# Mixed groups of 64 and 32 slots, and an earlier list of experts, in a hierarchical mixture of experts

## The chip, the cores and the metric

The kernel runs on one core of a Trainium2 chip. The metric is the device time of one execution in microseconds; lower is better. The profile divides the work of the core among TensorE (PE, with its weight loads PEld), VectorE (DVE), ScalarE (ACT), GpSimd (POOL) and SyncE (SP), whose sequencer issues the transfers this document speaks of.

## The reference

One block of a transformer for 512 tokens of width 1024: attention and a state space branch, an output projection with its residual, and a feed-forward part with 64 experts. The change lies in that last part. Each token picks one of 8 groups and in it 2 of 8 experts, so there are 1024 assignments; an expert is a gated unit of width 512:

```python
g_sel = jnp.argmax(g_logits, axis=-1)
e_sel_logits = jnp.take_along_axis(e_logits, g_sel[:, None, None], axis=1)[:, 0]
top_v, top_i = lax.top_k(e_sel_logits, MOE_TOP_K)          # 2 of 8
weights = g_gate[:, None] * jax.nn.softmax(top_v, axis=-1)
eid = g_sel[:, None] * MOE_EXPERTS_PER_GROUP + top_i
...
def expert_block(args):
    xblk, e = args
    hid = jax.nn.silu(xblk @ w_gate[e]) * (xblk @ w_up[e])
    return hid @ w_down[e]
```

All 64 experts' weights are fp32: gate and up 1024 x 512 each, down 512 x 1024, so 6 MB an expert and 384 MB in all.

## The kernel before

The time up to about 860 us goes to attention, the state space branch, the projections and the routing. Then the experts are worked through in groups. An expert has as many token slots as its place says: places 0 to 11 have 64 (the first four, the static ones, are experts 0 to 3; `NS`), places 12 to 63 have 32. The routing makes a list of the experts in the order of their counts (`perm`), so that the fuller ones come to the wide places; tokens beyond the slots are done by an overflow loop at the end. A group fills 128 columns of TensorE: a **pair** has two experts of 64, a **four** four of 32. The order is two pairs, six fours, four pairs, seven fours.

Per group, in TensorE's order: `gate_up` (8 k steps; in each, for gate and for up, one fp32 matmul of 512 columns for every expert, placed by `tile_position` on the expert's own columns of the array), `combine` of the group before (adds its weighted outputs to the tokens, 16 matmuls), `hidden_t` (4 transposes), `slots` of the next group (4 transposes and 4 small matmuls), and `down` (4 k steps of two halves). Every second group a `gather` of 64 matmuls stands ahead of `down`; it picks the token rows of the next two groups with the one-hot table P that `onehot` makes on VectorE. Group 0 and 1 are gathered together, piece by piece between the k steps of their own `gate_up`. In group 0 TensorE also makes the list (`counts`, at k = 4) and puts the routing weights into its order (`turn`, `put`).

The weights come by SP in loads of 1 MB (two k steps of gate and up, or of down, of one expert): six per expert, in the order of `tiles`, group by group, and inside a group by k step. A load needs a free buffer. `room` counts them; `done` sets the buffers of two k steps free when `gate_up` or `down` has issued these, and `fill` then issues as many loads as there is room for:

```python
def done(k, n=n):
    if k % 2:
        free(n)
        fill()
```

On the chip, a load waits until the matmuls have read its buffer. There are 19 buffers for these loads, and 17 from group 1 on (two become the accumulator). A load of an expert that is not static needs the list: SP reads its entry of `perm` (L1220) and then issues (L1252, or L1250 for a load in two halves).

Of the kernel before, what the change touches and what calls it, by code (L numbers as in the profile page):

```python
# [21 lines left out]
NCH = 4  # L22
# [96 lines left out]
def block_kernel(ctx: ExitStack, tc: tile.TileContext, I, out):  # L119
# [1082 lines left out]
    NS, NW, NF = 4, 12, 6  # L1202
    fours = [list(range(i, i + 4)) for i in range(NW, 64, 4)]
    pairs = [list(range(i, i + 2)) for i in range(0, NW, 2)]
# [19 lines left out]
    homes = []  # L1224
    room = {"ewx": 1, "stg": 0, "big": 0}

    def issue():
        n = nxt["i"]
        nxt["i"] += 1
        kind, e, q = tiles[n]  # L1230
        if n == 0:
            home = "ewx"
        elif n == XS:
            home = "stg"
        else:
            home = next(r for r in ("ewx", "stg", "big") if room[r] > (1 if r == "stg" and n < XS else 0))
        room[home] -= 1
        homes.append(home)
        if home == "stg":
            t = [stage(), stage()]  # L1240
        else:
            b = (mt("ewx", [128, 2048], "ew") if home == "ewx" else big("ew")).rearrange("p (k n) -> p k n", k=2)
            t = [b[:, 0], b[:, 1]]
        wt[kind, e, q] = t
        if n + LASTN >= len(tiles):
            return
        src = source(kind, e, q)
        if home == "stg":
            for i in range(2):
                nc.sync.dma_start(t[i], src[:, i])  # L1250
        else:
            nc.sync.dma_start(b, src)  # L1252
# [145 lines left out]
    def onehot(es, cs=range(NCH)):  # L1398
        n, w = len(es), E if es[0] < NW else E // 2
        if 0 in cs:  # L1400
            R["P", es[0]] = mt("P", [128, NCH, 256], "P")
        P = R["P", es[0]][:, :, :n * w]
        for c in cs:
            if es[0] == 0:
                for e in range(n):
                    V.tensor_scalar(P[:, c, e * w:e * w + w], iota1[:, :w], rk1[:, c, e:e + 1], fst[:, 3, c:c + 1],
                                    op0=OP.is_equal, op1=OP.mult)
            else:
                V.tensor_tensor(P[:, c].rearrange("p (e s) -> p e s", e=n),
                                rk1[:, c, es[0]:es[0] + n].unsqueeze(2).to_broadcast([128, n, w]),  # L1410
                                iota1[:, None, :w].to_broadcast([128, n, w]), op=OP.is_equal)
        if es[0]:
            scaled(P)
        return P
# [14 lines left out]
    def route(cl, prev):  # L1429
# [46 lines left out]
        def rk():  # L1476
            V.scalar_tensor_tensor(rk1[:, cs].rearrange("p c e -> p (c e)"), R["rps"][:, cl[0] * E:cl[-1] * E + E], 1.0,
                                   R["ab"][:, cs].rearrange("p c g e -> p (c g e)"), op0=OP.add, op1=OP.mult)
            R["P0"] = onehot(range(4), cl)

        def gat(k):
            if cl[0] == 0:
                gb[k] = side()
            gather_mm(R["P0"][:, :, :128], gb[k][:, :128], k, cl)
# [42 lines left out]

    def weights1():
        V.tensor_copy(R["cnt"], R["rps"][:, 256:256 + E])
# [19 lines left out]
    j = J("V", 0.8, weights1, [j, kj], prio=5, rel=["s"])  # L1549
# [5 lines left out]
    def free(n=1):  # L1555
        for _ in range(n):
            room[homes.pop(0)] += 1
# [15 lines left out]
    def order_tables():  # L1573


        ox = mt("y", [128, 1024], "ox")
        key, i64, w1, lt_ = (ox[:, i * E:i * E + E] for i in range(4))
        bd = ox[:, 512:640]
        kc, pc, cc_ = (ox[:, i:i + 1] for i in (640, 641, 642))
        tT = mt("y", [128, 4, 128], "tT")  # L1580
        V.tensor_scalar(key, R["cnt"], 64.0, None, op0=OP.mult)
        V.tensor_tensor(key, key, iota1, op=OP.subtract)
        V.tensor_scalar(key[:, :NS], iota1[:, :NS], -1.0, 1.0e6, op0=OP.mult, op1=OP.add)
        V.tensor_tensor(i64, ident[:, :E], ident[:, E:], op=OP.add)
        V.tensor_tensor(w1, key, i64, op=OP.mult)
        V.tensor_reduce(kc, w1, axis=AX.X, op=OP.add)
        V.tensor_scalar(lt_, key, kc, None, op0=OP.is_gt)
        V.tensor_reduce(pc, lt_, axis=AX.X, op=OP.add)
        V.tensor_scalar(pc, pc, 1.0, None, op0=OP.add)
        V.memset(bd, 0.0)  # L1590
        for i in range(2):
            r = slice(64 * i, 64 * i + 64)
            V.tensor_scalar(bd[r, 64 * i:64 * i + 64], iota1[r], pc[r], None, op0=OP.is_equal)
# [3 lines left out]
        def counts():  # L1597
            ps = side()
            T.matmul(ps[:1, :E], lhsT=pidx[:E], rhs=bd[:E, :E], start=True, stop=True)
            T.matmul(ps[:, E:2 * E], lhsT=cc_[:E].to_broadcast([E, 128]), rhs=bd[:E, :E], start=True, stop=True)  # L1600
            V.tensor_copy(R["perm"], ps[:1, :E])
            V.tensor_copy(R["cnt"], ps[:, E:2 * E])
# [13 lines left out]
        return {4: counts, 5: turn, 7: put}  # L1616
# [48 lines left out]
    def slots(P, n, w, wcols):  # L1665
        W = n * w
# [6 lines left out]
        for c in range(NCH):  # L1673
            T.matmul(ws[:W, :n], lhsT=P[:, c], rhs=wcols(c), start=(c == 0), stop=(c == 3))
        sl = pools["mp"].tile([128, 1], F32, name="sl", bufs=2)[:W]
        for e in range(n):
            V.tensor_scalar(sl[w * e:w * e + w], ws[w * e:w * e + w, e:e + 1], 0.5, None, op0=OP.mult)
        return pt, sl

    def gate_up(xt, n, w, gu, done=lambda k: None, pre=lambda k: None):  # L1680
        W = n * w
        pg, pu = gps.tile([128, 512], F32, name="g"), gps.tile([128, 512], F32, name="g")
        for k in range(8):
            pre(k)
            for i, o in enumerate((pg, pu)):
                for e in range(n):
# [18 lines left out]
    def down(ht, n, w, dn, done=lambda k: None):  # L1705
        ps = [side(), side()]
        for k in range(4):
            for i in range(2):
                for e in range(n):
                    es_ = slice(w * e, w * e + w)  # L1710
                    T.matmul(ps[i][es_], lhsT=ht[:, k, es_], rhs=dn(e, k)[:, i * 512:i * 512 + 512],  # L1711
                             start=(k == 0), stop=(k == 3), tile_position=(0, w * e))
            done(k)
        return ps
# [26 lines left out]

    def group_slots(P, gi):
        g_ = groups[gi]
        n, o = len(g_), 128 * (gi % 2)
        return slots(P[:, :, o:o + 128], n, 128 // n, lambda c: wtab[:, c, g_[0]:g_[0] + n])
# [4 lines left out]
    nP = [P]  # L1750
    for gi, g_ in enumerate(groups):
        n = len(g_)
        w = 128 // n
        last = gi == NG - 1

        def done(k, n=n):
            if k % 2:
                free(n)
                fill()

        def pre(k):
            if gi < 2 and 1 <= k < 7:
                half = slice(128 * gi, 128 * gi + 128)
                gather(P[:, :, half], xt[:, :, half], [k + 1])
            if gi == 0 and k in ordering:
                ordering[k]()
            if gi == 1 and k == 7:
                nP[0] = onehot(sum(groups[2:4], []))
# [3 lines left out]
        def wk(kind):  # L1772
            return lambda e, k: wt[kind, g_[e], k // 2][k % 2]
# [6 lines left out]
        o = 128 * (gi % 2)  # L1780
        hh = gate_up(xt[:, :, o:o + 128], n, w, wk("gu"), done, pre)
        if gi == 0:
            ps_ = group_slots(P, 0)
        elif not last:
# [7 lines left out]
        if gi % 2 == 0:  # L1792
            if not last:
                ps_ = group_slots(P, gi + 1)
            if gi == 0:
                gather(P[:, :, 128:], xt[:, :, 128:], [0, 1])
            elif gi + 2 < NG:
                nP[0] = onehot(sum(groups[gi + 2:gi + 4], []))
        elif not last:
            P = nP[0]  # L1800
            xt = rows(P.shape[2])
            gather(P, xt)
            ps_ = group_slots(P, gi + 1)
        yps = down(ht, n, w, wk("dn"), done)
# [7 lines left out]
    with tc.For_i(0, nov, 1) as m:  # L1812
# [23 lines left out]
        pt1, sl1 = slots(P1, 1, E, lambda c: cw1[:, c:c + 1])  # L1836
        hh = gate_up(xo, 1, E, lambda e, k: ow["gu", k])
# [3 lines left out]
        combine(pt1, *weighted(down(ht, 1, E, lambda e, k: ow["dn", k]), E, sl1, yo))  # L1841
# [123 lines left out]
```

## Time and profile before

| | |
|---|---|
| time, median of 3 runs | 1846.72 us (1846.01 to 1850.67) |
| the profiled execution | 1846.09 us, span in the trace 1844.3 us, mean granted TensorE clock 0.955 |
| TensorE busy | 1655.2 us (90%) |
| DMA | 474.68 MB, mean 257 GB/s over the span |
| expert loads, issue to landing | 18.3 us (gate/up), 18.6 us (down) |

The busy share is a mean over stages of different kinds. The page's line of GB/s, in 40 slices, shows where the stream of weights runs at its full rate and where it does not; a timeline of SP shows when loads are issued, and one of TensorE what it does between the reads that set buffers free.

### The profile page before, as it was taken

The page shows a single profiled execution, that of the slowest core. Times are in us where ns is not written, and L with a number is a line of the kernel's source. Part 1 is how long each engine was busy: PE and PEld are TensorE (multiplying, and loading weights), DVE is VectorE, ACT ScalarE, POOL GpSimd, SP SyncE. Part 2 cuts the span into 40 slices and gives each one's busy share as a digit, 9 for nine tenths or more (in the row PEclk, how much of TensorE's full clock was granted, in tenths as well). Part 3 has the DMA queues.
Part 4 walks back from the last instruction along what each step waited for, and adds up shares of the span by engine and source line. Part 5 has one row for each costly group of instructions (what it writes and reads, how often), then busy time and mean ns, then how long its engine had stood idle before and what let it go on. Part 6 is the DMA issues. An engine that isn't in the chain of part 4 may idle for free. (4 is left out here: it accounts for less than half of the span.)

```text
span 1844.3 us, 23121 instructions
## 1 busy us (share of the span) xinstructions
PE 1655.2 (90%) x8831; PEld 1033.7 (56%) x8831; DVE 788.4 (43%) x1499; ACT 424.8 (23%) x877; POOL 316.9 (17%) x329
## 2 busy tenths in 40 slices
PE   7999999999999999999996977769999787697775
PEld 6877788878787777887551423224455242142322
DVE  7698832587878865335230521021322212012113
ACT  5355530344444432121110100001111010010002
POOL 5244421253635352110000000000000000000001
PEclk9999999999999999999998998889999999898887
DMA  5321122212122122369869999999999999999994
GB/s 163 98 66 49 47 92 92 76 62 85 58 87 64 63 80 92 103 227 370 319 250 421 420 421 420 420 420 420 420 420 420 420 420 420 421 420 421 419 420 187
DMA packets 81329, 474.68 MB, mean 257 GB/s; under 512 B 10176, under 2 KB 10560, under 8 KB 35392
## 3 DMA queue, kind: packets, MB, share of 16 engines
q1 hardware_dynamic: 81216, 473.17, 64.9%
q8 instruction: 71, 1.16, 0.3%
q14 instruction: 42, 0.34, 0.1%
HBM read 471.04 MB, written 2.10 MB: 257 GB/s over the span
## 5 line engine op out<-in xcount | busy, mean ns | idle before, releaser
L1688 PE MATMUL g<-ew,xt 128*32 128x512 f32 (+1 forms) x1920 | 401.1, 691 | 131.8 <-DMA ew<-in_gu_dram 131.8
L243 PE MATMUL g<-hH,w 128*128 128x512 f32 x1024 | 345.7, 401 | 0.0
L1688 PEld LDWEIGHTS g<-ew,xt 128*32 128x32 f32 (+1 forms) x1920 | 96.0, 128 | 418.1 <-DMA ew<-in_gu_dram 237.6
L243 PEld LDWEIGHTS g<-hH,w 128*128 128x128 f32 x1024 | 192.4, 188 | 43.7 <-issue 5.9
L1693 DVE SCALAR_TENSOR_TENSOR hh<-hh,g 128x512 f32<-128x512 f32 x19 | 13.1, 688 | 457.4 <-ACT hh L1692 457.4
L243 PE MATMUL g<-hL,w 128*128 128x512 f32 x512 | 199.9, 390 | 0.0
L1711 PE MATMUL s<-ew,hT 128*32 128x512 f32 (+1 forms) x960 | 166.7, 640 | 20.2 <-DMA ew<-in_dn_dram 19.5
L1867 POOL TENSOR_TENSOR fst<-fst 128x1 f32<-128x1 f32 x4 | 1.2, 302 | 977.7 <-ACT fo L1860 977.7
L203 DVE TENSOR_TENSOR w<-stg,w 128x1024 fp32r<-128x1024 f32 x108 | 141.9, 1322 | 55.9 <-ACT w L200 33.2
L1422 PE MATMUL s<-P,x 128*128 128x256 f32 (+1 forms) x704 | 138.8, 355 | 0.0
L1422 PEld LDWEIGHTS s<-P,x 128*128 128x128 f32 x704 | 120.0, 192 | 24.2 <-issue 9.7
L1692 ACT ACTIVATE hh<-g 128x512 f32<-128x512 f32 x19 | 11.3, 597 | 476.2 <-PE g L1688 476.2
L198 POOL TENSOR_SCALAR w<-stg 128x1024 fp32r<-128x1024 f32 x60 | 70.5, 1175 | 255.0 <-DMA stg<-in_wu_dram 159.6
L1711 PEld LDWEIGHTS s<-ew,hT 128*32 128x32 f32 (+1 forms) x960 | 44.3, 121 | 125.0 <-issue 80.5
L243 PEld LDWEIGHTS g<-hL,w 128*128 128x128 f32 x512 | 96.4, 188 | 16.9
L1733 DVE TENSOR_TENSOR acc<-acc,s 128x512 f32<-128x512 f32 x144 | 88.0, 679 | 26.6 <-PE s L1728 26.6
L1721 DVE SCALAR_TENSOR_TENSOR yl<-s,sl,yh 128x512 fp32r<-128x512 f32 x38 | 28.5, 751 | 152.5 <-ACT yh L1720 151.1
L848 DVE SCALAR_TENSOR_TENSOR xb<-u,cw,xb 128x511 f32<-128x511 f32 (+2 forms) x96 | 81.7, 861 | 23.4 <-ACT xb L844 21.7
L243 PE MATMUL g<-w,hH 128*128 128x512 f32 x256 | 84.5, 411 | 0.0
L200 ACT ACTIVATE w<-stg 128x1024 fp32r<-128x1024 f32 x60 | 63.2, 1053 | 76.4 <-DMA stg<-in_wu_dram 53.8
L243 PE MATMUL g<-sH,w 128*128 128x512 f32 x256 | 80.0, 393 | 0.0
L1720 ACT ACTIVATE yh<-s,sl 128x512 fp32r<-128x512 f32 x38 | 26.1, 687 | 188.6 <-PE s L1711 187.5
(333 smaller groups left out, 2383.3 us busy)
## 6 DMA issues: line engine op xcount, KB each, us to landing
ew<-in_gu_dram SPq DMA_DIRECT2D x240, 1024.0 KB, 18.3
ew<-in_dn_dram SPq DMA_DIRECT2D x116, 1024.0 KB, 18.6
stg<-in_wu_dram SPq DMA_DIRECT2D x120, 512.0 KB, 3.6
stg<-in_gu_dram SPq DMA_DIRECT2D x32, 512.0 KB, 17.6
stg<-in_dn_dram SPq DMA_DIRECT2D x16, 512.0 KB, 17.4
xT<-in_xT_dram SPq DMA_DIRECT2D x4, 512.0 KB, 5.8
x<-in_xn_dram SPq DMA_DIRECT2D x2, 1024.0 KB, 10.9
ew<-in_dn_dram SPq DMA_DIRECT2D x4, 512.0 KB, 13.0
```

What stands on the lines that cost most here:

```text
L198: G.tensor_scalar(c["h"], c["st"], 1.0, 0.0, op0=OP.mult, op1=OP.add)
L200: A.activation(c["h"], c["st"], AF.Copy)
L203: (G if i % 10 == 9 else V).tensor_tensor(c["lo"], c["st"], c["h"].bitcast(F32), op=OP.subtract)
L243: T.matmul(cell[b], lhsT=x, rhs=y, start=first and i == 0, stop=last and i == 2)
L848: V.scalar_tensor_tensor(x()[:, 3 - k:], t["u"][:, :n], w[:, k:k + 1], x()[:, 3 - k:], op0=OP.mult, op1=OP.add)
L1422: T.matmul(o, lhsT=x1(c)[:, d], rhs=P[:, c], start=(c == 0), stop=(c == NCH - 1))
L1688: T.matmul(o[es_], lhsT=xt[:, k, es_], rhs=gu(e, k)[:, i * 512:i * 512 + 512], start=(k == 0), stop=(k == 7), tile_position=(0, w * e))
L1693: V.scalar_tensor_tensor(hh, hh, 1.0, pg[:W], op0=OP.add, op1=OP.mult)
L1711: T.matmul(ps[i][es_], lhsT=ht[:, k, es_], rhs=dn(e, k)[:, i * 512:i * 512 + 512], start=(k == 0), stop=(k == 3), tile_position=(0, w * e))
L1720: A.activation(yh[:, i], ps[i][:W], AF.Copy, scale=sl[:, :1])
L1721: V.scalar_tensor_tensor(yl[:, i], ps[i][:W], sl[:, :1], yh[:, i].bitcast(F32), op0=OP.mult, op1=OP.subtract)
L1733: V.tensor_tensor(res(c)[:, h], src(c)[:, h], ps, op=OP.add)
```

## The change

Every group but the first and the fours is now one expert of 64 slots and two of 32 (T below); the order is one pair, then T and F (a four) as the string says. Three experts are static. The list of experts is made by jobs of the routing (`order0` to `order2`) that TensorE and VectorE take before group 0. Buffers are set free by tile. Group 0 is gathered alone; the rows of groups 1 and 2 are gathered together between group 0's `down` and group 1's `gate_up`, and later gathers stand ahead of `down` in even groups.

```diff
-    NS, NW, NF = 4, 12, 6
-    groups = pairs[:NS // 2] + fours[:NF] + pairs[NS // 2:] + fours[NF:]
+    NS, NW = 3, 12
+    groups = [[0, 1]]
+    wide = list(range(2, NW))
+    for kind in "TFTFTTFTFTFTTFTFTF":
+        groups.append([wide.pop(0)] + some(2) if kind == "T" else some(4))
...
-        tiles += [("gu", e, q) for q in range(4) for e in g_] + [("dn", e, q) for q in range(2) for e in g_]
+        first = [e for e in g_ if e < NS]
+        for es in (first, g_[len(first):]):
+            tiles += [("gu", e, q) for q in range(4) for e in es] + [("dn", e, q) for q in range(2) for e in es]
...
+    def onehot(gs):
+        P = mt("P", [128, NCH, 256], "P")[:, :, :128 * len(gs)]
+        for i, g_ in enumerate(gs):
+            for w in (64, 32):
+                es = [e for e in g_ if width(e) == w]
+                if es:
+                    o = 128 * i + (128 - 32 * len(es) if w == 32 else 0)
+                    for c in range(NCH):
+                        V.tensor_tensor(P[:, c, o:o + w * len(es)].rearrange("p (e s) -> p e s", s=w),
...
+        scaled(P)
...
         def rk():
-            R["P0"] = onehot(range(4), cl)
+            for c in cl:
+                for e in range(2):
+                    V.tensor_scalar(R["P0"][:, c, 64 * e:64 * e + 64], iota1, rk1[:, c, e:e + 1], fst[:, 3, c:c + 1],
...
+    def order1():
+        V.tensor_copy(R["cnt"], R["rps"][:, 256:256 + E])
+        V.scalar_tensor_tensor(key, R["cnt"], 64.0, io, op0=OP.mult, op1=OP.subtract)
+        V.tensor_scalar(key[:, :NS], io[:, :NS], -1.0, 1.0e6, op0=OP.mult, op1=OP.add)
+        V.tensor_tensor(w1, key, i64, op=OP.mult)
+        V.tensor_reduce(kc, w1, axis=AX.X, op=OP.add)
+        V.tensor_scalar(lt_, key, kc, None, op0=OP.is_gt)
+        V.tensor_reduce(pc, lt_, axis=AX.X, op=OP.add)
+        for i in range(2):
+            r = slice(64 * i, 64 * i + 64)
+            V.tensor_scalar(ox[r, 512 + 64 * i:576 + 64 * i], io[r], pc[r], None, op0=OP.is_equal)
+
+    def order2():
+        R["ops"] = side()
+        T.matmul(R["ops"][:1, :E], lhsT=pidx[:E], rhs=R["ox"][:E, 512:576], start=True, stop=True)
...
+    oj = J("V", 1.8, order1, [kj, oj], prio=0.5, rel=["s"])
+    oj = J("P", 0.3, order2, [oj], prio=12, acq=["s"], lag=0.2)
+    J("V", 0.2, lambda: V.tensor_copy(R["perm"], R["ops"][:1, :E]), [oj], prio=0, rel=["s"], lag=0.2)
...
-    def free(n=1):
-        for _ in range(n):
-            room[homes.pop(0)] += 1
+    def free(tl_):
+        room[homes[tl_]] += 1
...
-        return {4: counts, 5: turn, 7: put}
+        return {3: turn, 5: put, 6: counts}
...
             for i, o in enumerate((pg, pu)):
-                for e in range(n):
-                    es_ = slice(w * e, w * e + w)
-                    T.matmul(o[es_], lhsT=xt[:, k, es_], rhs=gu(e, k)[:, i * 512:i * 512 + 512],
-                             start=(k == 0), stop=(k == 7), tile_position=(0, w * e))
+                for e, r in es:
+                    T.matmul(o[r], lhsT=xt[:, k, r], rhs=gu(e, k)[:, i * 512:i * 512 + 512],
+                             start=(k == 0), stop=(k == 7), tile_position=(0, r.start))
...
-            if gi < 2 and 1 <= k < 7:
-                half = slice(128 * gi, 128 * gi + 128)
-                gather(P[:, :, half], xt[:, :, half], [k + 1])
+            if gi == 0:
+                if 1 <= k < 7:
+                    gather(P, xt[:, :, :128], [k + 1])
...
         if gi == 0:
             ps_ = group_slots(P, 0)
+            P = onehot(groups[1:3])
...
+        if gi == 0:
+            xt = rows(256)
+            gather(P, xt)
+            ps_ = group_slots(P, 1)
```

`down` has the same edit as `gate_up`; `slots` now multiplies by 64 columns of the weight table where it took 2 or 4.

On TensorE, the end of the routing and the first k steps of group 0 before (L1422 are gathers, L1688 gate/up, L1599 makes the list):

```order
L303 MATMUL s<-ident 128x128 x4
L1422 MATMUL s<-P,x_7000 128x128 x4
L1688 MATMUL g<-ew,xt 64x512 x4
L1422 MATMUL s<-P,x_6945 128x128 x2
L1422 MATMUL s<-P,x_7000 128x128 x2
L1688 MATMUL g<-ew,xt 64x512 x4
...
L1599 MATMUL s<-ox,pidx 1x64
L1600 MATMUL s<-ox 128x64
L1688 MATMUL g<-ew,xt 64x512 x4
```

and of the change (L1436 gathers, L1715 gate/up, L1570 makes the list):

```order
L303 MATMUL s<-ident 128x128 x4
L1436 MATMUL s<-P,x_7000 128x128 x4
L1570 MATMUL s<-ox,pidx 1x64
L1715 MATMUL g<-ew,xt 64x512 x4
L1436 MATMUL s<-P,x_6945 128x128 x2
L1436 MATMUL s<-P,x_7000 128x128 x2
L1715 MATMUL g<-ew,xt 64x512 x4
```

The matmul that makes the list has moved from between the fourth and fifth k step of group 0 to ahead of the first.

On TensorE again, from group 0's down to group 1's gate/up, before (L1711 down, L1688 gate/up with gathers between its steps):

```order
L1711 MATMUL s<-ew,hT 64x512 x16
L1688 MATMUL g<-ew,xt 64x512 x4
L1422 MATMUL s<-P,x_6945 128x128 x2
L1422 MATMUL s<-P,x_7000 128x128 x2
L1688 MATMUL g<-ew,xt 64x512 x4
```

and of the change (L1737 down, L1436 gather, of which 16 such rows of 2 stand here, L1697 and L1702 the slots of group 1, L1715 gate/up):

```order
L1737 MATMUL s<-ew,hT 64x512 x16
L1436 MATMUL s<-P,x_6945 128x256 x2
L1436 MATMUL s<-P,x_7000 128x256 x2
...
L1697 MATMUL s<-ident,P 128x128 x4
L1702 MATMUL s<-ptab,P 128x64 x4
L1715 MATMUL g<-ew,xt 64x512
L1715 MATMUL g<-ew,xt 32x512 x2
L1715 MATMUL g<-ew,xt 64x512
L1715 MATMUL g<-ew,xt 32x512 x2
```

A whole gather for two groups has come between, and the matmuls of a k step change width twice per half.

On SP, the loads around the first read of the list, before:

```order
L1252 DMA ew<-in_gu_dram 128x2048 x8
L1252 DMA ew<-in_dn_dram 128x2048 x4
L1220 TENSOR_LOAD perm
L1252 ISA
L1252 DMA ew<-in_gu_dram 128x2048
L1220 TENSOR_LOAD perm
```

and of the change:

```order
L1270 DMA ew<-in_gu_dram 128x2048 x4
L1270 DMA ew<-in_dn_dram 128x2048 x2
L1238 TENSOR_LOAD perm
L1270 ISA
L1270 DMA ew<-in_gu_dram 128x2048
L1238 TENSOR_LOAD perm
```

Six loads of the fourth static expert are gone from ahead of the first read, which now follows 18 loads instead of 24.

## Rows read from the trace of the kernel before

**Rows 1.** The page: span, and GB/s in 40 equal slices of it.

```profile
span 1844.3 us, 23121 instructions
...
GB/s 163 98 66 49 47 92 92 76 62 85 58 87 64 63 80 92 103 227 370 319 250 421 420 421 420 420 420 420 420 420 420 420 420 420 421 420 421 419 420 187
```

**Rows 2.** Windows: length, busy us PE, PEld, DVE, ACT, POOL, clock, DMA share, GB/s.

```profile
864.00:963.00 99.00, 98.96 (x580) 53.23 (x577) 22.48 (x54) 15.87 (x33) 0.00 (x0) 1.00 0.69 270
948.00:1800.00 852.00, 701.74 (x3834) 292.85 (x3830) 180.33 (x351) 70.60 (x128) 0.00 (x0) 0.92 1.01 420
```

**Rows 3.** Waits of SP's queue, 862 to 948: total us, times, longest.

```profile
SPq L1252 <- PE g L1688: 46.6, 6, 17.6
SPq L1252 <- PE s L1711: 33.6, 4, 22.2
```

**Rows 4.** Timeline of SP, 785 to 950: start, us, issues of loads merged (xN).

```profile
817.08 2.49 SPq L1252 DMA_DIRECT2D ew<-in_gu_dram  x5
...
835.13 32.84 SPq L1252 DMA_DIRECT2D ew<-in_gu_dram  x8
868.06 12.73 SPq L1252 DMA_DIRECT2D ew<-in_dn_dram  x4
881.71 0.35 SPq L1252 DMA_DIRECT2D ew<-in_gu_dram  x1
...
909.16 37.64 SPq L1252 DMA_DIRECT2D ew<-in_gu_dram  x7
```

**Rows 5.** Timeline of TensorE, group 0: two k steps of gate/up.

```profile
862.72 1.94 PE L1688 MATMUL g<-ew,xt 128*64 128x512 f32 x8
...
865.68 1.94 PE L1688 MATMUL g<-ew,xt 128*64 128x512 f32 x8
```

**Rows 6.** Timeline of TensorE, groups 1 and 2: gather, down, gate/up of a four.

```profile
924.12 14.08 PE L1422 MATMUL s<-P,x 128*128 128x256 f32 x64
...
939.36 7.09 PE L1711 MATMUL s<-ew,hT 128*64 128x512 f32 x32
...
949.42 10.90 PE L1688 MATMUL g<-ew,xt 128*32 128x512 f32 x98
```

**Rows 7.** Timeline of VectorE: P and list of group 0, later P.

```profile
859.76 1.87 DVE L1406 TENSOR_SCALAR P<-iota,ptab,fst 128x64 f32<-128x64 f32 x8
...
866.46 0.53 DVE L1593 TENSOR_SCALAR ox<-iota,ox 64x64 f32<-64x64 f32 x2
...
916.17 1.43 DVE L1409 TENSOR_TENSOR P<-ptab,iota 128x256 f32<-128x256 f32 x4 [16.07 <-PE s L1422]
```

**Rows 8.** Transfers issued from 867 to 868: KB, us to landing.

```profile
ew<-in_gu_dram SPq DMA_DIRECT2D x1, 1024.0 KB, 4.7
```

**Rows 9.** Timeline of TensorE, 987 to 994.9, a four's k step that waits for loads.

```profile
989.72 1.04 PE L1688 MATMUL g<-ew,xt 128*32 128x512 f32 x2 [1.45 <-DMA ew<-in_gu_dram]
992.09 1.86 PE L1688 MATMUL g<-ew,xt 128*32 128x512 f32 x2 [1.32 <-DMA ew<-in_gu_dram]
994.58 1.08 PE L1688 MATMUL g<-ew,xt 128*32 128x512 f32 x4 [0.63 <-DMA ew<-in_gu_dram]
```

**Rows 10.** Timelines of TensorE and its weight loads, from pair to four.

```profile
944.56 1.89 PE L1711 MATMUL s<-ew,hT 128*64 128x512 f32 x8
946.38 0.62 PE L1688 MATMUL g<-ew,xt 128*32 128x512 f32 x1
...
945.42 0.14 PEld L1711 LDWEIGHTS s<-ew,hT 128*64 128x64 f32 x2 [0.28 <-issue]
946.37 0.11 PEld L1688 LDWEIGHTS g<-ew,xt 128*32 128x32 f32 x1 [0.81 <-issue]
```

**Rows 11.** Timeline of weight loads, the two other changes of width.

```profile
1286.90 0.13 PEld L1688 LDWEIGHTS g<-ew,xt 128*64 128x64 f32 x1 [0.84 <-issue]
...
1422.64 0.11 PEld L1688 LDWEIGHTS g<-ew,xt 128*32 128x32 f32 x1 [0.81 <-issue]
```

**Rows 12.** Weight loads at the change from group 0's down to group 1.

```profile
897.96 0.14 PEld L1688 LDWEIGHTS g<-ew,xt 128*64 128x64 f32 x2 [0.29 <-issue]
```

More of the change, by code (lines that the diff above doesn't have):

```diff
@@ L1197, in block_kernel, with some, width, spans @@
     give("big", 8, [wsl])
-    NS, NW, NF = 4, 12, 6
-    fours = [list(range(i, i + 4)) for i in range(NW, 64, 4)]
-    pairs = [list(range(i, i + 2)) for i in range(0, NW, 2)]
-    groups = pairs[:NS // 2] + fours[:NF] + pairs[NS // 2:] + fours[NF:]
-    NG = len(groups)
+    NS, NW = 3, 12
+    narrow = iter(range(NW, 64))
+    def some(n):
+        return [next(narrow) for _ in range(n)]
+    groups = [[0, 1]]
+    wide = list(range(2, NW))
+    for kind in "TFTFTTFTFTFTTFTFTF":
+        groups.append([wide.pop(0)] + some(2) if kind == "T" else some(4))
+    NG = len(groups)
+    def width(e):
+        return 64 if e < NW else 32
+    def spans(g_):
+        o = 0
+        for e in g_:
+            yield e, slice(o, o + width(e))
+            o += width(e)
     tiles = []
     for g_ in groups:
-        tiles += [("gu", e, q) for q in range(4) for e in g_] + [("dn", e, q) for q in range(2) for e in g_]
+        first = [e for e in g_ if e < NS]
+        for es in (first, g_[len(first):]):
+            tiles += [("gu", e, q) for q in range(4) for e in es] + [("dn", e, q) for q in range(2) for e in es]
     wt = {}
@@ L1237, in issue @@
         room[home] -= 1
-        homes.append(home)
+        homes[kind, e, q] = home
         if home == "stg":
@@ L1598, in counts @@
             ps = side()
[L1599 to L1602, printed above, removed]
+            T.matmul(ps[:, :E], lhsT=cc_[:E].to_broadcast([E, 128]), rhs=bd[:E, :E], start=True, stop=True)
+            V.tensor_copy(R["cnt"], ps[:, :E])
         def turn():
@@ L1663, in rows, with slots @@
         return mt("xt", [128, 8, 256], "xt")[:, :, :w]
-    def slots(P, n, w, wcols):
-        W = n * w
+    def slots(P, es, wcols):
+        W = es[-1][1].stop
         ps = side()
@@ L1673, in slots, with gate_up @@
         for c in range(NCH):
[L1674 removed]
+            T.matmul(ws[:W, :E], lhsT=P[:, c], rhs=wcols(c), start=(c == 0), stop=(c == 3))
         sl = pools["mp"].tile([128, 1], F32, name="sl", bufs=2)[:W]
[L1676 to L1677 removed]
+        for e, r in es:
+            V.tensor_scalar(sl[r], ws[r, e:e + 1], 0.5, None, op0=OP.mult)
         return pt, sl
[L1680 to L1681 removed]
+    def gate_up(xt, es, gu, done=lambda k: None, pre=lambda k: None):
+        W = es[-1][1].stop
         pg, pu = gps.tile([128, 512], F32, name="g"), gps.tile([128, 512], F32, name="g")
@@ L1703, in hidden_t, with down @@
         return ht
-    def down(ht, n, w, dn, done=lambda k: None):
+    def down(ht, es, dn, done=lambda k: None):
         ps = [side(), side()]
@@ L1708, in down @@
             for i in range(2):
[L1709 to L1712, printed above, removed]
+                for e, r in es:
+                    T.matmul(ps[i][r], lhsT=ht[:, k, r], rhs=dn(e, k)[:, i * 512:i * 512 + 512],
+                             start=(k == 0), stop=(k == 3), tile_position=(0, r.start))
             done(k)
@@ L1740, in combine, with cols @@
                 combine_add(combine_mm(pt, yh, yl, c, i), c, i, src)
+    def cols(gi):
+        o = 128 * ((gi + 1) % 2) if gi else 0
+        return slice(o, o + 128)
     def group_slots(P, gi):
-        g_ = groups[gi]
-        n, o = len(g_), 128 * (gi % 2)
-        return slots(P[:, :, o:o + 128], n, 128 // n, lambda c: wtab[:, c, g_[0]:g_[0] + n])
+        return slots(P[:, :, cols(gi)], list(spans(groups[gi])), lambda c: wtab[:, c])
     xt, P = xt[0], R["P0"]
@@ L1749, in block_kernel @@
     ordering = order_tables()
-    nP = [P]
     for gi, g_ in enumerate(groups):
-        n = len(g_)
-        w = 128 // n
         last = gi == NG - 1
[L1756 to L1759, printed above, removed]
+        es = list(spans(g_))
         def pre(k):
-            if gi < 2 and 1 <= k < 7:
-                half = slice(128 * gi, 128 * gi + 128)
-                gather(P[:, :, half], xt[:, :, half], [k + 1])
[L1765 to L1768, printed above, removed]
+            if gi == 0:
+                if 1 <= k < 7:
+                    gather(P, xt[:, :, :128], [k + 1])
+                if k in ordering:
+                    ordering[k]()
             elif last and k == 4:
@@ L1772, in wk, with done, f @@
         def wk(kind):
-            return lambda e, k: wt[kind, g_[e], k // 2][k % 2]
+            return lambda e, k: wt[kind, e, k // 2][k % 2]
+        def done(kind):
+            def f(k):
+                if k % 2:
+                    for e in g_:
+                        free((kind, e, k // 2))
+                    fill()
+            return f
         if last:
@@ L1791, in block_kernel @@
         pt, sl = ps_
[L1792 to L1801, printed above, removed]
+        if gi % 2:
+            ps_ = group_slots(P, gi + 1)
+            if not last and gi + 2 < NG:
+                P = onehot(groups[gi + 2:gi + 4])
+        elif gi and not last:
+            xt = rows(256)
             gather(P, xt)
             ps_ = group_slots(P, gi + 1)
-        yps = down(ht, n, w, wk("dn"), done)
+        yps = down(ht, es, wk("dn"), done("dn"))
+        if gi == 0:
+            xt = rows(256)
+            gather(P, xt)
+            ps_ = group_slots(P, 1)
         pend = (pt, *weighted(yps, 128, sl))
```

66 lines of the change are left out of this document (24 added, 42 removed).

## The prediction

> **What bounds the kernel now.** I read the page first, for where the span goes. In its GB/s line (40 slices of 46.1 us) slices 22 to 39 stand at 419 to 421, and the three before them at 370, 319 and 250 [rows 1]. So the second half of the span is the stream of expert weights, and TensorE, busy as it looks, waits for it. The windows say how tight that is: from 948 to 1800 the stream moves 420 GB/s, but between 864 and 963 only 270, while TensorE is busy without a gap at a granted clock of 1.00 [rows 2]. One load of 1 MB (1.0486 million bytes) at 420 GB/s takes 2.50 us. The lull is worth 99 x (1 - 270/420) = 35.4 us of stream, and as all 384 MB must pass, this idle time is what the end waits for; the rest of the stage can't be shortened by TensorE.
>
> Next, who holds the loads back in the lull: between 862 and 948 SP waits 46.6 us for TensorE's gate/up matmuls and 33.6 for its down matmuls, that is, for a buffer to be read out, and not for the list of experts [rows 3]. One load goes out early and eighteen from 817.1 on without a pause; the last of the eight issues from 835.1 to 868.0 is the twentieth, which waits until 867.6, and the run of seven that starts at 909.2 holds the longest pause [rows 4]. TensorE is slow there because it does other work between reads: in group 0 the gathers stand between the k steps (a step is 2.96 us, of it 1.9 gate/up) [rows 5]; after group 1 come combine, a 14.1 us gather for two groups, and only then the down matmuls that free buffers [rows 6].
>
> **The change, part by part.** *Loads.* Bytes, count and size stay: 384 loads. So only idle stream time counts, and the sum is: the profiled execution's 1846.1 us (1.8 outside its span of 1844.3, 0.6 under the median of 1846.7), less 35.4, plus the new idle time.
>
> *List of experts.* Load 19 now needs the list. VectorE makes four compares for P instead of eight from 859.76 on (half of 1.87 us) and then nine short operations; their like took 0.26 us each, so I count 2.2 us [rows 7]: list ready 862.9, TensorE's one matmul, which now stands ahead of group 0, at about 863.1, group 0 at 863.4 instead of 862.7, the copy at 864.0, SP's read and issue 0.9 to 1.3 us on (880.8 to 881.7 is the like case [rows 4]): issued 865.3. A load into an idle queue lands 4.7 us after its issue [rows 8]: 870.0, where 866.8 would be its turn (817.1 + 4.7 + 18 x 2.50). Below, this costs nothing (if it arrives in time); above, 16 us more, if it went out no sooner than the first such load of before (881.7 [rows 4]). I take 3.2, since nothing else stands on that path.
>
> *Group 0* reads two experts as before. Half of its gather is gone from behind its gate/up, but a gather of 14.1 us and the slots (1.4) for groups 1 and 2 now stand between its down and group 1. Steps at 2.96, with the moved table work: gate/up ends 886.9, down 889.9 to 896.8 (7 us as before), gather to 910.9, group 1 at 912.2. VectorE's one-hot tables for that gather are twelve compares and a product; four compares took 1.43 us [rows 7], so I count 5; they lie beside the down matmuls, and each microsecond beyond 896.8 would be a microsecond of delay.
>
> *Groups of 64 + 32 + 32 (call them T).* This decides. Widths that are alike run beside each other: a pair of 64, or four of 32, takes 0.43 us per pass (98 matmuls of a four in 10.9 us [rows 6]). An expert's two passes follow each other: at 989.7 both ran before the next expert's weights landed at 992.1 [rows 9]. No row shows 64 and 32 on different columns at once. The ends: side by side, a half step (512 columns, two passes) is 0.86 us, as for pairs; one after the other, it is the wide expert's two passes, then the narrow two's. The nearest rows are the three places where the width changes between groups. At 946.38 the first 32-wide matmul starts 0.53 us after the last pass of the 64-wide (rounds at 944.56, 944.99, 945.42, 945.85), not 0.43; and its weights are loaded at 946.37, right ahead of it, where the 64-wide ones had theirs one whole pass earlier (945.42 for 945.85) [rows 10]. The same stands at 1422.64 and 1286.90, where the weight loads had been idle for 0.81 and 0.84 us [rows 11], against 0.28 between rounds, while from 64 to 64 the weights at 897.96 were early [rows 12]. In these places the columns overlap, which a T group's don't; but the early loading ends too, so I take it that TensorE finishes one width before it takes up the other. Then a half step is 0.52 + 0.43 + 0.52 + 0.43 = 1.90 us, a T's gate/up (16) 30.5, its down (8) 15.2, in all 25.1 more than side by side.
>
> The Trainium skill's "TensorEngine Tiling (Array Packing)", section Key Properties, says that changing the tiling mode, not just the tile, drains the TensorE. By that rule the sum stays as it is here, since 128x64 and 128x32 are listed as modes of their own; the rows at the three changes agree with it, with 0.10 us (0.53 less 0.43) at 946.38, but only for overlapping columns.
>
> *What a group costs TensorE besides.* Four pair groups took 1286.90 to 1422.64 = 135.7 us with two gathers [rows 11]: (135.7 - 28.2)/4 = 26.9, of it 20.6 matmuls; 6.4 are combine, transposes and slots. So T is 52 us, and its three experts need 18 x 2.50 = 45 us of stream; F is 27, or 41 with a gather, against 60.
>
> *New idle time, followed through the order of the loads.* (1) Load 18 lands at 864.3. Load 33 is the first that group 1's gate/up frees, at its second k step: 912.2 + 4 x 1.90 = 919.8, landed 924.5. Fourteen loads (35 us) lie in these 60.2: 25.2 idle. (2) Group 1's gate/up frees twelve buffers, two of which become the accumulator; its last is read at 942.7, and the first down buffers come after 6.4 + 7.6 us, at 956.7, landed 961.4. Ten loads from 924.5 are done by 947.0; 961.4 - 2.5 - 947.0 = 11.9 idle. (3) Two T's follow each other twice (groups 5 and 6, 12 and 13). From the end of group 4 to the first down buffer of group 6: 52 + 30.5 + 20.4 (combine and gather) + 7.6 = 110.5 us. In this the stream can place 17 buffers plus the 30 that are read, less 4 already landed (12 loads fit into the F's last 31 us, 8 of them its own): 43 loads, 107.5 us. With the 2.2 us of latency: 5 idle. Bounds 0 and 29 (118 of TensorE less 90 of stream for 36 loads). I take 6, and 4 for the second time. (4) Issue gaps of the old lull, some 2. Sum 25.2 + 11.9 + 10 + 2 = 49.1, that is 13.7 more than 35.4: **1846.1 + 13.7 = 1859.8, forecast 1860 us**, slower by 0.7%. Its own range is 1850 (both doubles free, list in time) to 1875 (doubles at half their bound).
>
> **Rivals.** *Side by side (faster).* If disjoint columns of different width run together, group 1 frees load 33 at 912.2 + 4 x 0.86 = 915.6, landed 920.3: 56.0 - 35 = 21.0 idle. Its down buffers come at 912.2 + 13.7 + 6.4 + 3.4 = 935.7, ahead of the stream (945.3), so no idle there, and a T (27, with a gather 41) is under its 45. With 2 of gaps: 23, so 1846.1 - 12.4 = 1834. For it: column groups ran independently at 994.58, where four started together though one of them was the rest of an older round [rows 9]. Against it: the early weights that stop at each change of width. It decides at a half step of about 1.7 us; below this the gain remains. The Trainium skill's "TensorE: Matmul & The Clock Gate", Part 3, The mechanism, has the tile's place in a mask per instruction and lets tiles that don't conflict overlap; read so, it speaks for this rival and would make 1834; rows 9 agree for equal widths and no row shows unequal ones.
>
> *TensorE bounds the whole stage (much slower).* If buffers take up less of the double T's than I count, up to 29 us each come back as idle: 1846.1 + (25.2 + 11.9 + 58 + 2 - 35.4) = 1908. Against it: 17 buffers are 42 us deep, and in the pair stage a group took TensorE 33.9 us (135.7/4 [rows 11]) for 30 us of stream, and the mean over 948 to 1800 is still 420 GB/s [rows 2].
>
> *Nothing measurable.* One width still ends before the other but the next width's weights load early, or the list costs and the smaller lull gains cancel: within 5.5 us of 1846.
>
> **How the numbers follow.** One width after the other as summed 0.52; side by side 0.36; TensorE-bound beyond 1876 0.07; no change 0.05. What this kernel's measurement can tell from no change is about 0.3% (5.5 us). The range reaches from side by side with the list in time (1830) to the doubles at half their bound (1876): it leaves out the TensorE-bound case and some of the edges. Faster: 0.36 and a little of the forecast's and the null's low side, 0.38; same 0.06; slower 0.56.
>
> **What would show it.** In a T group, the 32-wide matmuls start about 0.95 us after the 64-wide one (0.43 + 0.52) and 0.01 us after it if the rival holds; gate/up of group 1 lasts 30 us or 14. The stream's lull ends near 962 with a second dip inside group 1, or near 920. In groups 5 to 6 TensorE is without gaps and SP waits for it. Group 0 starts within 1 us of 862.7 and load 19 is issued near 865. The prediction is wrong if T's half step is not near 1.9 us, or if the gather ahead of group 1 waits for VectorE's tables.

## The result, and the profile after

The change took 1859.42 us (median, 1855.86 to 1861.72) against 1847.57 us for the kernel before on the same chip: a ratio of 1.006, 95% interval 1.0038 to 1.0082, so it is slower by about 12 us. The profiled execution is the fastest of the four, 1855.86 us with a span of 1854.1.

The page of the changed kernel: the span, TensorE's share, and GB/s in 40 slices of 46.4 us.

```profile
span 1854.1 us, 23043 instructions
...
PE 1792.5 (97%) x8767; PEld 1034.0 (56%) x8767; DVE 794.3 (43%) x1566; ACT 422.2 (23%) x869; POOL 317.6 (17%) x329
...
GB/s 158 101 63 52 47 91 91 80 58 91 61 77 74 64 71 100 103 248 367 245 313 421 420 420 420 420 339 421 420 420 420 420 421 415 374 420 420 421 420 255
```

Beside [rows 1], the old lull (367, 245, 313) is there still, and two slices later in the stream have fallen to 339 and 374, which stood at 420. TensorE has gone to 97% busy, though it has 8767 matmul passes where the kernel before has 8831. Windows over these places (us, busy PE, PEld, DVE, ACT, POOL, clock, DMA share, GB/s), of the changed kernel:

```profile
864.00:970.00 106.00, 105.31 (x484) 43.24 (x484) 21.91 (x64) 12.12 (x24) 0.00 (x0) 1.00 0.72 277
970.00:1780.00 810.00, 788.99 (x3576) 289.13 (x3564) 176.84 (x395) 70.07 (x126) 0.00 (x0) 0.99 1.00 413
1140.00:1240.00 100.00, 99.75 (x436) 35.32 (x438) 19.13 (x44) 8.33 (x15) 0.00 (x0) 1.00 0.93 382
1530.00:1620.00 90.00, 89.75 (x393) 29.03 (x392) 19.71 (x42) 7.04 (x12) 0.00 (x0) 1.00 0.97 394
```

and of the kernel before, the same two long stretches:

```profile
864.00:970.00 106.00, 105.87 (x634) 56.87 (x632) 29.39 (x69) 16.46 (x34) 0.00 (x0) 1.00 0.71 280
970.00:1780.00 810.00, 663.19 (x3578) 277.86 (x3576) 165.87 (x324) 69.41 (x126) 0.00 (x0) 0.92 1.01 420
```

Idle stream, at 420 GB/s: in the lull 106 x (1 - 277/420) = 36.1 us against 35.3, and behind it 810 x (1 - 413/420) = 13.5 us against none. So the lull was not shortened and two new dips came. Why, TensorE's timeline of a k step in group 1 shows (start, us, merged matmuls):

```profile
936.97 1.62 PE L1715 MATMUL g<-ew,xt 128*64 128x512 f32 x3
937.98 0.62 PE L1715 MATMUL g<-stg,xt 128*32 128x512 f32 x1
938.42 0.59 PE L1715 MATMUL g<-ew,xt 128*32 128x512 f32 x1
938.43 0.59 PE L1715 MATMUL g<-stg,xt 128*32 128x512 f32 x1
938.95 1.07 PE L1715 MATMUL g<-ew,xt 128*64 128x512 f32 x2
```

and the timeline of its weight loads in the same stretch:

```profile
936.97 0.19 PEld L1715 LDWEIGHTS g<-ew,xt 128*64 128x64 f32 x2 [0.84 <-issue]
937.97 0.11 PEld L1715 LDWEIGHTS g<-ew,xt 128*32 128x32 f32 x1 [0.81 <-issue]
...
938.95 0.19 PEld L1715 LDWEIGHTS g<-ew,xt 128*64 128x64 f32 x2 [0.84 <-issue]
```

The 64-wide pass starts at 936.97, the 32-wide ones of the other columns 1.01 us later, the next 64-wide at 938.95: a half step takes 1.98 us, and no pass of one width runs beside one of the other. The weights of each width are loaded only when the other has ended, after the 0.81 and 0.84 us of idle time that [rows 10, 11] show at the old changes of width.

The lull itself is read from these points of the changed kernel. On TensorE they are the start of group 0, the start of group 1's gate/up, and the first matmul behind it:

```profile
862.99 1.98 PE L1715 MATMUL g<-ew,xt 128*64 128x512 f32 x8
...
911.16 25.44 PE L1715 MATMUL g<-ew,xt 128*64 128x512 f32 x75
...
942.92 0.50 PE L1753 MATMUL s<-yh,pt 128*128 128x512 f32 x1
```

On SP they are the issue of load 19, the first that needs the list, and of the first load whose buffer group 1 frees:

```profile
864.43 0.36 SPq L1270 DMA_DIRECT2D ew<-in_gu_dram  x1
...
919.21 2.01 SPq L1270 DMA_DIRECT2D ew<-in_gu_dram  x3
```

Counted from the first load, the one issued at 919.21 is the 32nd, since the 19 buffers and the twelve that group 0 frees hold 31. The prediction and an expectation below call it load 33. The fourteen loads that the prediction counts behind load 18 end at load 32, so its sum is not changed by this.

### The profile page after: what moved, and what is told of

Same layout as the page of the kernel before. It is cut to its first block, busy times and chain, and to the rows that moved or that the text cites. A ratio compares the mean times of both kernels' runs of the same rounds, so it can differ in the third digit from the quotient of the medians.

```text
span 1854.1 us, 23043 instructions
## 1 busy us (share of the span) xinstructions
PE 1792.5 (97%) x8767; PEld 1034.0 (56%) x8767; DVE 794.3 (43%) x1566; ACT 422.2 (23%) x869; POOL 317.6 (17%) x329
## 5 line engine op out<-in xcount | busy, mean ns | idle before, releaser
L1715 PE MATMUL g<-ew,xt 128*32 128x512 f32 (+1 forms) x1904 | 460.3, 603 | 13.4 <-DMA ew<-in_gu_dram 13.3
L1715 PEld LDWEIGHTS g<-ew,xt 128*32 128x32 f32 (+1 forms) x1904 | 91.9, 114 | 348.5 <-issue 319.0
L1737 PE MATMUL s<-ew,hT 128*32 128x512 f32 (+1 forms) x968 | 245.2, 634 | 13.4 <-DMA ew<-in_dn_dram 12.0
L1737 PEld LDWEIGHTS s<-ew,hT 128*32 128x32 f32 (+1 forms) x968 | 49.2, 119 | 193.7 <-issue 150.9
L1436 PE MATMUL s<-P,x 128*128 128x256 f32 (+1 forms) x640 | 136.3, 372 | 0.0
L1436 PEld LDWEIGHTS s<-P,x 128*128 128x128 f32 x640 | 117.3, 192 | 20.8 <-issue 5.7
L1719 ACT ACTIVATE hh<-g 128x512 f32<-128x512 f32 x19 | 11.3, 597 | 425.1 <-PE g L1715 425.1
## 6 DMA issues: line engine op xcount, KB each, us to landing
ew<-in_dn_dram SPq DMA_DIRECT2D x4, 512.0 KB, 13.7
```

The lines of the kernel that those rows point to most:

```text
L1436: T.matmul(o, lhsT=x1(c)[:, d], rhs=P[:, c], start=(c == 0), stop=(c == NCH - 1))
L1715: T.matmul(o[r], lhsT=xt[:, k, r], rhs=gu(e, k)[:, i * 512:i * 512 + 512], start=(k == 0), stop=(k == 7), tile_position=(0, r.start))
L1737: T.matmul(ps[i][r], lhsT=ht[:, k, r], rhs=dn(e, k)[:, i * 512:i * 512 + 512], start=(k == 0), stop=(k == 3), tile_position=(0, r.start))
```

## The experiments

Two columns below come from the landing times of all expert loads in each profile: how much longer the time from the second landing to the last is than 2.49 us for each 1 MB between them (the stream's idle time, the lull in it), and the time from the last landing to the end of the span (the tail). The difference of two rows says more than a row by itself, which depends on the 2.49. Ratios are to runs of the kernel before on the same chip.

| run | median us | ratio, 95% interval | stream idle | tail |
|---|---|---|---|---|
| before | 1847.57 | | 44.1 | 25.0 |
| the change | 1859.42 | 1.006, 1.0038 to 1.0082 | 59.2 | 20.1 |
| e1_split32 | 1829.11 | 0.9908, 0.9892 to 0.9923 | 31.2 | 20.1 |
| e2_width_once | 1846.38 | 0.9998, 0.9989 to 1.0007 | 47.8 | 20.1 |
| e3_list_only | 1847.53 | 1.0007, 0.9998 to 1.0016 | 46.5 | 24.5 |
| e4_no_mixed | 1835.16 | 0.9935, 0.9921 to 0.9949 | 38.3 | 20.1 |
| e5_late_list | 1826.76 | 0.9888, 0.9872 to 0.9905 | 29.7 | 20.1 |
| e6_gather_halves | 1824.23 | 0.9876, 0.9860 to 0.9893 | 26.7 | 21.2 |
| e7_one_double | 1868.52 | 1.0120, 1.0103 to 1.0136 | 58.3 | 33.3 |

**Is it the width? (e1_split32)** The wide expert is issued as two tiles:

```diff
+    def cuts(es):
+        m = min(r.stop - r.start for e, r in es)
+        return [(e, slice(o, o + m)) for e, r in es for o in range(r.start, r.stop, m)]
...
-                for e, r in es:
+                for e, r in cuts(es):
                     T.matmul(o[r], lhsT=xt[:, k, r], rhs=gu(e, k)[:, i * 512:i * 512 + 512],
```

> The change, with the wide expert of a T group issued as two tiles of 32 columns beside the two of its narrow experts, so that every tile of a T group is 32 wide; columns, data and order are the same, and TensorE gets a third more matmuls. Theory (tiles of different width don't run beside each other, and that is the whole loss): a half step of a T falls from 1.98 us to about 0.86, group 1's gate/up from 31.8 us to about 14, the load that waits longest in the lull is issued near 915.6 rather than 919.2, the dips near 960 and 1225 go, and the time is 1834 to 1838. Rival (the loss comes from the gather that stands ahead of group 1, or from loads in an order that suits T badly): the half step may fall, but the time stays above 1850.

Measured: 1829.11, some 30 us under the change and 17 under the kernel before. TensorE's timeline of group 1 and of the first gate/up of group 2:

```profile
909.89 10.93 PE L1719 MATMUL g<-ew,xt 128*32 128x512 f32 x99
...
929.91 7.07 PE L1741 MATMUL s<-ew,hT 128*32 128x512 f32 x64
936.80 7.05 PE L1719 MATMUL g<-ew,xt 128*32 128x512 f32 x64
```

The 32 matmuls of the down, 64 passes, take 7.07 us, which is 16 rounds of 0.43, where the change takes 8 half steps of 1.98. The load that waits longest goes out at 913.59, ahead of the 915.6 expected:

```profile
913.59 1.18 SPq L1270 DMA_DIRECT2D ew<-in_gu_dram  x2
```

In the page of this run no slice between the lull and the last one is under 419 GB/s. The same data in the same columns, with a third more matmuls in the T groups, runs side by side once all tiles have one width. So the mixed widths cost the change 28 us by the ratios and by the idle time (30 by the medians), more than the whole loss. The time is 5 us under the expectation: that was made from the sum for the rival, which left the tail out (below).

**How is a change of width priced? (e2_width_once)**

```diff
-            for i, o in enumerate((pg, pu)):
-                for e, r in es:
+            for w in sorted({r.stop - r.start for e, r in es}, reverse=True):
+              for i, o in enumerate((pg, pu)):
+                for e, r in [x for x in es if x[1].stop - x[1].start == w]:
```

> The change, with each k step of a T group issued by width: the wide expert's gate and up, then the narrow two's (down likewise), so that the width changes 2 times in a k step and not 4. Theory (one width after the other, and at each change 0.13 us more than between two passes): a k step falls from 3.96 us to about 3.70, the time by 3 to 8 us, to 1852 to 1857. Rival (widths could run together, and only the order of issue keeps them apart): the k step falls toward 2 us and the time to 1840 or below.

Weight loads of a k step of group 1 in this run:

```profile
918.63 0.19 PEld L1716 LDWEIGHTS g<-ew,xt 128*64 128x64 f32 x2 [0.84 <-issue]
919.11 0.14 PEld L1716 LDWEIGHTS g<-ew,xt 128*64 128x64 f32 x1 [0.29 <-issue]
919.54 0.14 PEld L1716 LDWEIGHTS g<-ew,xt 128*64 128x64 f32 x1 [0.29 <-issue]
920.49 0.14 PEld L1716 LDWEIGHTS g<-ew,xt 128*32 128x32 f32 x4 [0.81 <-issue]
...
922.33 0.19 PEld L1716 LDWEIGHTS g<-ew,xt 128*64 128x64 f32 x2 [0.84 <-issue]
```

A k step is 922.33 - 918.63 = 3.70 us, eight passes of 0.43 and two changes of 0.13, as the theory had it; the widths still don't run together. But the time fell by 13 us (11.5 by the ratios), not by 3 to 8. The rest is in the dips, which these windows of the run show at 403 and 420 GB/s instead of 382 and 394:

```profile
1140.00:1240.00 100.00, 99.91 (x460) 40.13 (x463) 21.84 (x49) 8.92 (x16) 0.00 (x0) 1.00 0.98 403
1530.00:1620.00 90.00, 89.91 (x463) 37.65 (x460) 19.84 (x45) 8.10 (x15) 0.00 (x0) 1.00 1.02 420
```

At 420 GB/s that is 5.0 and 5.6 us of stream. I read it so, without a run that shows it: a dip is what TensorE needs beyond the stream's lead in buffers, so what is taken from TensorE there comes off the dip whole, until it is gone.

**Is the early list worth anything? (e3_list_only, e5_late_list)** The first puts `order0` to `order2` and their jobs, as the change has them, into the kernel before.

> The kernel before, with the list of experts made within the routing and nothing else of the change. Theory (the lull is made by buffers that are read late, and the list only stands beside that): within 3 us of the kernel before; group 0 starts some 0.5 us later. Rival (loads after the 24th waited for the list too): faster by 5 us or more.

The interval holds 1, so the list alone is worth nothing that shows. (Group 0 began 2.3 us later than in the kernel before, at 865.00, and not 0.5.) The second takes the early list back out of e1_split32:

```diff
-    oj = J("P", 0.3, order2, [oj], prio=12, acq=["s"], lag=0.2)
...
+            T.matmul(ps[:1, E:2 * E], lhsT=pidx[:E], rhs=bd[:E, :E], start=True, stop=True)
+            V.tensor_copy(R["perm"], ps[:1, E:2 * E])
...
-        return {3: turn, 5: put, 6: counts}
+        return {3: turn, 5: put, 4: counts}
```

> As the kernel with the wide expert as two tiles of 32, but the matmul that makes the list stands in group 0 at the fifth k step again, as in the kernel before; loads 19 on are issued after it. Theory (between load 18 and load 33 only the first buffer that group 1 frees counts, and the fourteen loads between them have 12 us to spare): load 19 lands near 881 instead of 868, loads 20 to 32 follow without a pause, load 33 lands where it did (919.5), and the time stays within 2 us of 1829, so the early list is worth nothing here. Rival (the early list is what T groups with three static experts live on): 8 to 13 us slower.

SP's timeline of that run:

```profile
878.00 5.52 SPq L1270 DMA_DIRECT2D ew<-in_gu_dram  x7
885.57 2.05 SPq L1268 DMA_DIRECT2D stg<-in_gu_dram  x2
888.20 9.26 SPq L1270 DMA_DIRECT2D ew<-in_dn_dram  x4
898.04 21.71 SPq L1270 DMA_DIRECT2D ew<-in_gu_dram  x5
```

Load 19 goes out at 878.0, where e1_split32 had it at 863.2. The twelve loads behind it (thirteen issues, one load being in two halves) follow with 1.3 us of idle stream between them, and there is still an idle wait of 5.5 us ahead of load 32, where e1_split32 has 12.2. The ratio, 0.9888, lies just under the interval of e1_split32's (0.9892 to 0.9923), and the two intervals overlap; the median is 2.3 us under 1829.11, a little outside the 2 us expected. So the late list is not slower, and the rival's 8 to 13 us are ruled out. As the theory said, only load 32, the first whose buffer group 1 frees, ends the lull.

**What is the rest of the change worth? (e4_no_mixed)**

```diff
-    NS, NW = 3, 12
+    NS, NW = 4, 12
...
-    for kind in "TFTFTTFTFTFTTFTFTF":
-        groups.append([wide.pop(0)] + some(2) if kind == "T" else some(4))
+    for kind in "PFFFFFFPPPPFFFFFFF":
+        groups.append([wide.pop(0), wide.pop(0)] if kind == "P" else some(4))
```

> The change, with the groups of before (two pairs, six fours, four pairs, seven fours, four static experts): the early list, group 0 gathered alone, and the gathers where the change has them, but no group of mixed width. Theory (mixed widths cost some 25 us and the rest of the change gives back about 12): 1834 to 1839, with the stream's lull over near 940. Rival (the rest of the change brings nothing, since the gather ahead of group 1 holds buffers back as long as the gathers between its steps did): 1844 to 1850.

Measured 1835.16, 11.3 us under the kernel before. The time is as expected, the reason only by half: the stream's idle time is 5.8 us shorter, not 12, and 4.9 us come from a shorter tail, which no theory had named. On the same chip e1_split32 is 6.0 us faster than this run: with tiles of one width, groups of 64 + 32 + 32 (with three static experts) beat the pairs and fours of before, and the loss lay in the mixed widths and not in the mixed groups.

**Does the gather set the end of the lull? (e6_gather_halves)** On top of e1_split32:

```diff
+            if gi == 1:
+                gather(P[:, :, 128:], xt[:, :, 128:])
...
-            gather(P, xt)
+            gather(P[:, :, :128], xt[:, :, :128])
             ps_ = group_slots(P, 1)
```

> As the kernel with the wide expert as two tiles of 32, but only the rows of group 1 are gathered ahead of it, and those of group 2 ahead of the down matmuls of group 1. Theory (the lull ends when group 1's gate/up frees its first buffer): that comes about 6 us earlier (8.1 us of gather instead of 14.1), of which a dip of some 1 to 2 us inside group 1 takes a part: 4 to 6 us faster than 1829. Rival (the time that leaves the first lull comes back whole inside group 1, where 8 us of gather are added ahead of the down matmuls): within 1.5 us of 1829.

TensorE between group 0's down and the gate/up of group 1, in this run:

```profile
896.09 7.41 PE L1436 MATMUL s<-P,x 128*128 128x128 f32 x64
...
904.71 10.93 PE L1719 MATMUL g<-ew,xt 128*32 128x512 f32 x99
```

Gate/up starts 5.2 us earlier than the 909.89 of e1_split32, and the idle time is 4.6 us less, with 2.4 us (two waits of 1.2) in the new dip inside group 1. It is the fastest of all, 1824.23, or 1.2% under the kernel before. That is 4.9 us under 1829.11, as expected, but e1_split32 ran on another chip; against e5_late_list on the same chip, which differs from e1_split32 by the list, it is only 2.5 us faster. So it goes the way of the theory, and the size stays open between 2.5 and 5 us. The gather does set the end of the lull: load 32 goes out at 908.41, against 913.59 in e1_split32.

**Do adjacent T's make the dips? (e7_one_double)** The order is `"TFTFTFTFTFTTFTFTFT"`.

> The change with its groups in another order, so that T groups follow each other once (groups 11 and 12) instead of twice and the last group is a T. Theory (mixed widths make TensorE fall behind the stream where two T's are adjacent, 8.5 us and 5.7 us of idle stream in the profile of the change): the dips near 1225 and 1590 go and one comes near 1480, of 5 to 9 us; 5 to 9 us faster than the change, 1850 to 1855. Rival (the loss lies in every T alike): no difference, 1857 to 1861, and small gaps of the stream at many T's.

This one was missed: 1868.52. The places were right in kind: no dip near 1225, and a single one behind the only adjacent pair, around 1540 (1480 expected), none at T's that stand alone, so the rival falls too:

```profile
1140.00:1240.00 100.00, 94.00 (x456) 35.37 (x452) 20.37 (x46) 8.33 (x15) 0.00 (x0) 1.00 1.02 420
1530.00:1620.00 90.00, 85.25 (x401) 24.05 (x400) 19.49 (x44) 4.98 (x8) 0.00 (x0) 0.98 0.90 370
```

But the dip is 12.1 us (9.9, 1.2 and 1.1 at the loads that land from 1543.96 to 1563.58), nearly as much as the two of the change together (8.5 + 5.7), and I can't say from the rows why one dip is so much deeper. And the last group is a T now: its matmuls run on behind the last load, which puts 13.2 us on the tail (33.3 against 20.1); the expectation had left that out.

**Where the tail comes from (w8_shift, w12_shift, w20_shift)** These are the kernel before with 8, 12 and 20 filler matmuls (`keep_warm`) instead of 4 ahead of the overflow loop, which this data skips.

> The kernel before with 8 instead of 4 filler matmuls of TensorE ahead of the overflow loop, which is skipped; this asks about the 5.3 us that TensorE stands before its first matmul behind that loop in the kernel before, where the change shows 1.8 us. Theory (how much code has to be loaded behind the loop depends on where it stands in memory): with the program of TensorE moved by a few instructions, one of the three shifts shows about 1.8 us and one load of instructions in the gap instead of two. Rival (the gap belongs to the work of the kernel before): about 5 us less the 0.5 us of filler, and two loads, in all three.

> As the run with 8, with 12 filler matmuls. The same two theories: 1.8 us and one load of instructions in the gap in at least one of the three, or about 5 us less 0.9 us and two loads in all.

> As the run with 8, with 20 filler matmuls. The same two theories: 1.8 us and one load of instructions in the gap in at least one of the three, or about 5 us less 1.9 us and two loads in all.

TensorE's timeline behind the loop, kernel before:

```profile
1820.34 1.16 PE L303 MATMUL s<-ident 128*128 128x128 f32 x8
1826.81 0.79 PE L1727 MATMUL s<-yh,pt 128*128 128x512 f32 x1 [5.31 <-issue]
```

with 12 fillers:

```profile
1820.35 2.94 PE L303 MATMUL s<-ident 128*128 128x128 f32 x24
1825.10 0.52 PE L1727 MATMUL s<-yh,pt 128*128 128x512 f32 x1 [1.81 <-issue]
```

and in the changed kernel:

```profile
1835.03 1.16 PE L303 MATMUL s<-ident 128*128 128x128 f32 x8
1837.94 0.50 PE L1753 MATMUL s<-yh,pt 128*128 128x512 f32 x1 [1.75 <-DVEq L1839]
```

The gap is 4.92 us with 8 fillers, 1.81 with 12 and 1.66 with 20. The DMA view of the gap (queue, packets, MB, share) has two loads of instructions on queue q8 in the kernel before, as with 8 fillers:

```profile
q8 instruction: 2, 0.03, 2.4%
```

and one with 12 fillers, as with 20 and in the change:

```profile
q8 instruction: 1, 0.02, 3.3%
```

In the kernel before, the granted clock behind the gap is 0.50, the lower of its two levels (1.2 GHz), after TensorE had stood for 5.31 us; in the changed kernel, after 1.75 us, it is 1.00, the upper one (2.4 GHz). These are windows of the combine, the matmuls behind the loop:

```profile
1826.80:1831.60 4.80, 4.79 (x11) 3.79 (x12) 2.88 (x5) 2.43 (x7) 0.92 (x3) 0.50 0.00 0
```

```profile
1838.00:1842.00 4.00, 3.87 (x16) 2.87 (x16) 3.29 (x6) 2.57 (x9) 0.92 (x3) 1.00 0.00 0
```

With 12 fillers the same stretch of the combine stands at 0.60, so the clock does not follow from the gap alone. The work behind the loop is the same in the kernel before and in these three, so the long gap does not belong to it. Longer fillers by themselves don't end it either: with 8 of them the first matmul of the combine starts 7.0 us after the first filler, with 4 it is 6.5 and with 12 it is 4.8. That the place of the code in memory sets the gap fits this, as the theory said, but no run shows the place itself. e3_list_only has 4.86 us, and the six experiments built on the change have 1.75 to 1.83, though their programs differ in length ahead of the loop. Each of these three had one execution, so of their times nothing is said.

## Why the prediction was right, and where it was not

The forecast was 1860 us, and the time 1859.42. Its steps:

*Widths* (the step that decides): right. I had 0.95 us from one width to the other and a half step of 1.90; it is 1.01 and 0.97, together 1.98, and gate/up of group 1 lasts 31.8 us (30.5 forecast). e1_split32 shows that this is the cause of the whole loss: the rival's 1834, less the 4.9 us of the tail, is about what comes out once the widths agree (1829.11). The Trainium skill's "TensorEngine Tiling (Array Packing)", Key Properties, says that a change of tiling mode drains TensorE. The trace now agrees for columns that don't overlap as well: 128x64 and 128x32 take 1.98 us a half step, where tiles of one width take 0.86. The Trainium skill's "TensorE: Matmul & The Clock Gate", Part 3, The mechanism, lets tiles overlap, and names a row group that does not conflict, or the background weight buffer, as the condition. Here all tiles have the same 128 rows; they overlap in e1_split32, where they have one width (16 rounds in 7.07 us), and in the change those of different width do not.

*Lull.* Right. Load 19 was issued at 864.4 (865.3 forecast), group 0 began at 862.99 (863.4), group 1 at 911.2 (912.2); the gather ahead of it did not wait for VectorE's tables. The load that ends the pause, called load 33 and in truth load 32, was issued at 919.2 and took 4.8 us to land (919.8 and 924.5 forecast). The idle time from load 18 up to it is 24.6 us (25.2), and from there to the first load that group 1's down frees 11.4 (11.9). In the changed kernel the early list is no cause: the lull's length follows from two points, load 18 and load 32, as the sum had it. e5_late_list shows that the 3.2 us I took for the list was no term of it at all.

*Adjacent T's*: mis-sized, 8.5 + 5.7 = 14.2 us against 6 + 4, and e7_one_double shows that I can't size them: one such place cost 12.1. Each is the small difference of two large sums, so an error of 0.08 us in a half step, 48 half steps to a double, gives 4 us.

*The sum.* New idle time was forecast at 13.7 us more than before and came to 15.0. The profiled execution is only 9.8 us longer, since the tail is 4.9 us shorter and the stream begins 0.3 us earlier. The tail was in no term and in no rival, and it is not the widths' doing: e4_no_mixed has the same 20.1 us without mixed widths. That the median of the change stands 3.6 us above its profiled execution (that of the kernel before 1.5) brought the time back to the forecast: that they agree within 1 us is luck. The upper end of the range has a slip: with both doubles at half their bound of 29, its own terms give 1846.1 + (25.2 + 11.9 + 29 + 2 - 35.4) = 1878.8 and not 1875 or 1876. The result is far from it.

*Chances.* I gave 0.36 to widths that run side by side, since in all rows of before the columns overlapped where the width changed. The sign that decided was there: weight loads that come early while the width stays, and late when it changes.

## What to carry to other kernels

In these runs column tiles, 128x64 and 128x32 in fp32, shared TensorE only while they had one width. Where shapes must be mixed, try to cut the wide tile into tiles of the narrow width, even if TensorE then gets more matmuls for the same data. When a stream of loads is the bound, follow which buffer ends each pause. Work that is made earlier, as the list here, is worth nothing if the load that it frees is not that one. And the last dozen microseconds of a span deserve a row of their own in the sum.

## What was not expected of the hardware

TensorE stood 5.3 us behind a skipped loop or 1.8: two pieces of instructions were loaded on queue q8 in the gap or one. Eight more small matmuls ahead of the loop were enough to go from the one to the other, four more were not. That the place of the program in memory decides it is argued and not shown. In the kernel before TensorE then ran most of the combine at the lower clock (0.43 us a matmul instead of 0.23), which with the gap makes up the 4.9 us of the tail (3.6 of it the gap). What lets the clock fall there is open: behind the short gaps it was low in part with 12 fillers (0.60) and in e6_gather_halves (0.57 over the first 4 us of the combine, which is why its tail is 21.2), and not with 20 (0.23 us a matmul from the second one on).
